# Turned outputs a piece a step, token factors on ScalarE and other orders of loads, in a hybrid mLSTM and DeltaNet block

## The chip, the cores and the metric

One Trainium2 chip, one of its cores. The time is device microseconds (us) of one execution. Before the change the runs took 2233.39, 2235.78 and 2241.74 us, a median of 2235.78.

## The reference

One decoder layer on 512 tokens of width 2048, all in fp32. The two input streams of heads and the merge come from one projection each way:

```python
u = rmsnorm(x, norm_w)
z = u @ w_in                  # q, k, v, gates of mLSTM; q, k, v, gates of DeltaNet; merge gates
h_ml = mlstm(...)             # 8 heads, qk 128, v 256, chunkwise; gated, normalised per head
h_dn = gated_delta(...)       # 16 heads of 128; conv of 4 taps, SiLU, l2norm of q and k, decay
y_ml, y_dn = h_ml @ w_out[:2048], h_dn @ w_out[2048:]
out = rmsnorm(x + sigmoid(g1) * y_ml + sigmoid(g2) * y_dn, final_norm_w)
```

The DeltaNet heads need in each chunk the solution of a lower triangular system (1 + A) X = R, where A is made of the products of the keys, of the decays and of a factor per token.

## The kernel before

**Products.** Each fp32 operand is split into a part that TensorE takes exactly (hi, L135 on ScalarE) and the rest (lo, L138 on VectorE), and each product takes three matmuls: hi hi, hi lo, lo hi. The lines are L261 to L263 in `proj_cm`, L575 to L577 in `seven` and L1306 to L1308 in the wide blocks. Weights come in 256 KB tiles by SP's DMA queue (`wr`, L176), four raw and four split buffers (`wh`, `wl`), split three weights ahead of their use.

**Steps.** TensorE's order is written out by hand. After every six wide matmuls the program calls `tick()`, which advances all the side work, written as Python generators: each `yield n` says that the generator goes on n ticks later, and `start(gen, n)` puts one in. A scheduler puts the other engines' instructions into the order of each engine by priority: `urgent` raises it, and `behind("A")` (or "V", "S") ties an instruction behind the newest split on ScalarE (VectorE), or behind the newest weight load on SP. Each engine then works in order.

**Stages.** (1) 0 to 95 us: x, the norm, u transposed and split. (2) To about 1050: `seven`, a scheme of seven products of half size for eight, in twelve blocks of 77 us. A block has quads A, then quads B; each quad is three weight tiles of 512 columns (`load_quad`, L505, in `wr3`) of which VectorE makes sums. An A quad writes its sum ts to DRAM (`t2_d`, L531), and the B quad of the same rows reads it back as the third of its three tiles and makes `ts = r[0] - r[2]` (L535). (3) 1060 to 1960: eight DeltaNet units of two heads, with the mLSTM heads between them. A unit projects k, v, q (`proj_cm`, copied out by `conv_silu` into `yp`, L770), makes the matrices of the solve (`dn_front_k`), sends them over DRAM (`ld`, `ls`) to the 32x32 layout, runs 31 steps of substitution on VectorE (`tmp`, L881), completes the inverse by four products with copies by ScalarE and VectorE between them (`dn_back`, p1 to p4; the copy of p3 is `s`, L962, which L966 multiplies), then runs the chain over the chunks (`dn_chain`, L990 to L1011). (4) To 2010: the third wide block, with `load_h2`, which loads and splits the DeltaNet outputs, and `lead`, which loads three quads of the next stage and splits the first. (5) 2011 to 2172: two blocks of `seven` for the output projection, whose sums stand in `t2o_d`. (6) To 2232: `last_block`, with the mLSTM outputs (`hmr`, split to `uh` and `ul` by L1180 and L1181), the known parts of y (`hf`, L1427), their squares (L1435) and the final norm.

**Turned outputs.** `turn` transposes a head's output in 32x32 blocks on VectorE into a buffer `to` (two of them), and `travel` sends it to DRAM (`hm_d`, `h_d`) in four pieces of 64 KB (L806). Outputs go by ScalarE's DMA queue, all four pieces in one step; loops inside a unit go by SP's queue. An mLSTM head has two outputs, one step apart.

**Token factors.** Three tiles are multiplied by a factor per token in one VectorE instruction of 128x512 each: `aq` by `cs` (L857, ahead of the solve), `vt` by `nk` (L972, ahead of the chain), `kw` by `we` (L1110, mLSTM).

Of the kernel before, what the change touches and what calls it, by code (L numbers as in the profile page):

```python
# [11 lines left out]
ALU = mybir.AluOpType  # L12
# [3 lines left out]
P = 128  # L16
S = 512
NC = S // P
# [9 lines left out]
YDRAIN = 2  # L28
# [14 lines left out]
BS = 32  # L43
# [12 lines left out]
def hybrid_body(  # L56
# [27 lines left out]
    tg_d = dr.tile([NC, P, 2 * D], F32, tag="tgd", name="tg_d")  # L84
# [47 lines left out]
    newest = {}  # L132
# [7 lines left out]
    def behind(eng):  # L140

        return tc.issue_after(newest[eng])
# [66 lines left out]
    def urgent(level=1):  # L209
        return tc.high_priority(offset=level * PRIO)  # L210
# [6 lines left out]
    def start(gen, wait=0, by=None):  # L217
        active.append([gen, clock["t"] + wait, held["by"] if by is None else by])
# [29 lines left out]
    banks = (((psj, "pj"),) * 3 + ((psw, "wk"),), ((psw, "wk"),) * 2 + ((pso, "o"),) * 2)  # L248
# [235 lines left out]
    def seven_stage(sbp, su, s4, X, t2_d, w_, k0, blocks, sinks, hook):  # L484
# [8 lines left out]
        def load_quad():  # L493
            if len(rawq) == len(quads):
                return
            _, c1, c2, b, g, i = quads[len(rawq)]
            with tc.high_priority(offset=2 * PRIO):
                r = sbp.tile([P, 3, NO], F32, tag="wr3", name="wr3", bufs=3)
                k1, k2 = (slice((k0 + 2 * i + n) * P, (k0 + 2 * i + n + 1) * P) for n in range(2))
                if g == "A":  # L500
                    src = (w_[k1, c1:c1 + NO], w_[k1, c2:c2 + NO], w_[k2, c2:c2 + NO])
                else:
                    src = (w_[k2, c1:c1 + NO], w_[k2, c2:c2 + NO], t2_d[b % 2, i])
                for n in range(3):
                    nc.sync.dma_start(r[:, n, :], src[n])  # L505
            rawq.append(r)

        def split(src, wide):
# [217 lines left out]
    lead, seven = seven_stage(sbp, (suh, sul), (s4h, s4l), X, t2_d, w_in, 0, SEVEN, SINK, begin_mixers)  # L726
# [36 lines left out]
    def bc(col, n):  # L763
        return col.unsqueeze(2).to_broadcast([P, NC, n])
# [27 lines left out]
    def turn(src, dst, out=False, lag=5):  # L792


        o = dst if dst is not src and len(dst.shape) == 3 else wk.tile([P, NC, P], F32, tag="to", name="to", bufs=2)
        V.transpose(o if len(src.shape) == 3 else o.rearrange("p n c -> p (n c)"), src)
        start(travel(o, dst, out), lag if out else 2)

    def travel(o, dst, out):

        d = dst if len(dst.shape) == 4 else dr.tile([16, BS, 4, BS], F32, tag="td", name="td", bufs=8)
        ov = o.rearrange("p n (j c) -> p (n j) c", c=BS)
        q = nc.scalar if out else nc.sync
        with behind("A") if out else urgent(2):
            for a in range(4):
                q.dma_start(d[:, :, a, :].rearrange("m r c -> r m c"), ov[a * BS:(a + 1) * BS])  # L806
        if d is dst:
            return
        yield 4
        with behind("A") if out else urgent(2):  # L810
            q.dma_start(dst, d.rearrange("(n j) r a c -> (j r) n (a c)", n=NC))
        yield 1

    def dn_front_k(hs, kq, u):
# [37 lines left out]
            V.tensor_tensor(out=cs[:, j, :], in0=cs[:, j, :], in1=beta[:, :, hs[j]], op=ALU.mult)  # L852
        u["nk"] = nk
        ld = dr.tile([2 * NC, 4, BS, BS], F32, tag="ld", name="ld", bufs=2)
        for j in range(2):
            aq = u["aq"][j]
            V.tensor_tensor(out=aq[:, :, 0, :], in0=aq[:, :, 0, :], in1=bc(cs[:, j, :], P), op=ALU.mult)  # L857
# [65 lines left out]
    def dn_back(hs, kq, u):  # L923

        tn, tt = u["tn"], u["tt"]
        G2 = [(j * NC + c, u["aq"][j][:, c, 0, :]) for j in range(2) for c in range(NC)]
        for b in range(4):
            bs = slice(b * BS, (b + 1) * BS)
            G.tensor_copy(tb[bs, :, bs], tt[bs])
        for b in range(2):  # L930
            bs = slice(b * BS, (b + 1) * BS)
            G.tensor_copy(ta[bs, :, bs], tn[bs])
        p1 = psw.tile([P, 2 * NC, BS], F32, tag="wk", name="p1")
        for g, a in G2:
            for q in range(2):
                a0, a1 = slice(64 * q, 64 * q + 32), slice(64 * q + 32, 64 * q + 64)
                T.matmul(p1[a1, g, :], a[a0, a1], tn[a0, g, :], start=True, stop=True)
        s1 = wk.tile([P, 2 * NC, BS], F32, tag="s3", name="s1", bufs=1)
        for q in range(2):
            a1 = slice(64 * q + 32, 64 * q + 64)  # L940
            with urgent():
                A.mul(s1[a1], p1[a1], -1.0)
        yield 2
        p2 = psw.tile([P, 2, 2 * NC, BS], F32, tag="wk", name="p2")
        for g, a in G2:
            for q in range(2):
                a0, a1 = slice(64 * q, 64 * q + 32), slice(64 * q + 32, 64 * q + 64)
                T.matmul(p2[a0, 0, g, :], s1[a1, g, :], tt[a1, g, :], start=True, stop=True)
            T.matmul(p2[32:64, 1, g, :], tt[32:64, g, :], s1[32:64, g, :], start=True, stop=True)
        with urgent(2):  # L950
            V.tensor_copy(ta[32:64, :, 0:32], p2[32:64, 1])
        for q in range(2):
            a0, a1 = slice(64 * q, 64 * q + 32), slice(64 * q + 32, 64 * q + 64)
            with urgent():
                A.copy(tb[a0, :, a1], p2[a0, 0])
        yield 3
        p3 = psw.tile([P, 2 * NC, 64], F32, tag="wk", name="p3")
        for g, a in G2:
            T.matmul(p3[64:128, g, :], a[0:64, 64:128], ta[:, g, :], start=True, stop=True)
        s3 = wk.tile([P, 2 * NC, 64], F32, tag="s3", name="s3", bufs=1)  # L960
        with urgent():
            A.mul(s3[64:128], p3[64:128], -1.0)  # L962
        yield 2
        p4 = psw.tile([P, 2 * NC, 64], F32, tag="wk", name="p4")
        for g, a in G2:
            T.matmul(p4[0:64, g, :], s3[64:128, g, :], tb[64:128, g, 64:128], start=True, stop=True)  # L966
        with urgent():
            V.tensor_copy(tb[0:64, :, 64:128], p4[0:64])
        for j in range(2):
            vn = u["vs"][j]  # L970
            with behind("V"):
                V.tensor_tensor(out=vn, in0=vn, in1=bc(u["nk"][:, j, :], P), op=ALU.mult)  # L972
        start(dn_chain(0, hs, kq, u), 2)
        start(dn_chain(1, hs, kq, u), 3)

# [99 lines left out]
    def ml_head(h, kq):  # L1075
# [30 lines left out]
        G.memset(v1[:, :, NB:NB + 1], 1.0)  # L1106
        nc.sync.dma_start(v1[:, :, 0:NB], v_d[:, :, h * NB:(h + 1) * NB].rearrange("c p n -> p c n"))
        yield 6
        with behind("V"):
            V.tensor_tensor(out=kw, in0=kw, in1=bc(we, P), op=ALU.mult)  # L1110
        yield 2

        sq = wk.tile([P, NC], F32, tag="sq", name="sq")
# [257 lines left out]
    X2 = late["X"]  # L1371
# [52 lines left out]
        return (lambda t: put(tgs[11, t], m1[t], t, c1)), end5, end7  # L1424

    def known(c, a, b):
        nc.sync.dma_start(fin["hf"][:, c, a:b], y_d[c, :, a:b])  # L1427

    def put(t, src, c, col, now=True):
        gated(t, src, now)  # L1430
# [94 lines left out]
    def last_block():  # L1525
# [30 lines left out]
        def beside():  # L1556
            yield 2
            for c in range(NC):
                known(c, 0, HD)
                yield 2  # L1560
            nc.sync.dma_start(fw, final_norm_w.partition_broadcast(P))
            yield 2
            for c in range(NC):
                known(c, HD, D)
                nc.sync.dma_start(tgs[c], tg_d[c, :, nsl])
                for n, a in enumerate(range(0, HD, NO)):
                    square(c, a, a + NO, n)
                weigh(c, 0, HD)
                yield 3
                square(c, HD, CT, 2)  # L1570
                weigh(c, HD, CT)
                yield 1
# [34 lines left out]
                    tick()  # L1607
            done_c(c)

    wide_block(YDRAIN, banks[1], lambda c: X2[:, c // 2, c % 2, :], [(load_h2(), 1), (lead(), 18)])  # L1610
    for b, blk in enumerate(OUTS):
        seven(2 * KH * b, *blk)
    last_block()
# [33 lines left out]
```

## Time and profile before

| | |
|---|---|
| runs | 2233.39, 2235.78, 2241.74 us |
| profiled execution | 2233.9 us, span 2232.1 us |
| TensorE | busy 2159.3 us, 97%, mean granted clock 0.994 |
| VectorE | busy 1671.0 us, 75% |
| ScalarE | busy 995.0 us, 45% |
| GpSimd | busy 276.6 us, 12% |
| DMA | 435.81 MB, mean 195 GB/s |

A row of the waits names the waiting instruction, who it waited for, the total, how often and the longest, in us. A row of a timeline has the start, the duration, the engine (ACTq and SPq are DMA issues), the line, the operation and, in brackets, the idle time before it with its releaser. A row of the windows has the stretch, its length, the busy times of TensorE, its weight loads, VectorE, ScalarE and GpSimd with their counts, the granted TensorE clock, the DMA share and GB/s. A row of the groups has the line, engine, operation, shapes and count, the busy us and the mean ns of one, and the idle time before. The profile was taken on one execution; times in it start at the span's start.

### The profile page before, as it was taken

The page shows a single profiled execution, that of the slowest core. Times are in us where ns is not written, and L with a number is a line of the kernel's source. Part 1 is how long each engine was busy: PE and PEld are TensorE (multiplying, and loading weights), DVE is VectorE, ACT ScalarE, POOL GpSimd, SP SyncE. Part 2 cuts the span into 40 slices and gives each one's busy share as a digit, 9 for nine tenths or more (in the row PEclk, how much of TensorE's full clock was granted, in tenths as well). Part 3 has the DMA queues.
Part 4 walks back from the last instruction along what each step waited for, and adds up shares of the span by engine and source line. Part 5 has one row for each costly group of instructions (what it writes and reads, how often), then busy time and mean ns, then how long its engine had stood idle before and what let it go on. Part 6 is the DMA issues. An engine that isn't in the chain of part 4 may idle for free. (4 is left out here: it accounts for less than half of the span.)

```text
span 2232.1 us, 31548 instructions
## 1 busy us (share of the span) xinstructions
PE 2159.3 (97%) x10592; PEld 1771.9 (79%) x10592; DVE 1671.0 (75%) x2907; ACT 995.0 (45%) x1890; POOL 276.6 (12%) x356
## 2 busy tenths in 40 slices
PE   7999999999999999999999999999999999999997
PEld 5877878888788788788878887878888887877775
DVE  5787788888878777877588876757675868667875
ACT  5444444444444343444544544444444445344344
POOL 0320000000000000000222422222222211110101
PEclk9999999999999999999999999999999999999999
DMA  5456666667667766776776767676756568695896
GB/s 156 125 174 193 199 201 201 205 202 231 197 208 228 235 210 205 229 244 192 195 189 168 179 145 174 147 172 166 178 139 167 141 153 230 186 278 184 250 317 215
DMA packets 534821, 435.81 MB, mean 195 GB/s; under 512 B 241921, under 2 KB 393698, under 8 KB 534530
## 3 DMA queue, kind: packets, MB, share of 16 engines
q1 hardware_dynamic: 425058, 357.68, 56.4%
q10 hardware_dynamic: 105568, 68.77, 9.8%
q0 software_dynamic: 4032, 7.34, 2.2%
q8 instruction: 83, 1.36, 0.3%
q14 instruction: 80, 0.66, 0.1%
HBM read 342.37 MB, written 95.49 MB: 196 GB/s over the span
## 5 line engine op out<-in xcount | busy, mean ns | idle before, releaser
L135 ACT CAST wh<-wr 128x512 fp32r<-128x512 f32 (+1 forms) x538 | 379.9, 707 | 470.9 <-PE pj L262 261.8
L138 DVE TENSOR_TENSOR wl<-wr,wh 128x512 fp32r<-128x512 f32 (+1 forms) x538 | 447.2, 834 | 178.2 <-ACT wh L135 160.2
L261 PE MATMUL pj<-uh,wh 128*128 128x512 f32 x1024 | 431.6, 421 | 4.2 <-ACT yp L770 4.2
L263 PE MATMUL pj<-uh,wl 128*128 128x512 f32 x1024 | 404.3, 395 | 0.0
L262 PE MATMUL pj<-ul,wh 128*128 128x512 f32 x1024 | 403.2, 394 | 0.0
L576 PE MATMUL ps<-wl,uh 128*128 128x512 f32 x704 | 277.3, 394 | 7.2 <-DVE wl L138 7.0
L575 PE MATMUL ps<-wh,uh 128*128 128x512 f32 x704 | 276.3, 392 | 7.0 <-DVE X L617 6.5
L577 PE MATMUL ps<-wh,ul 128*128 128x512 f32 x704 | 275.0, 391 | 0.0
L135 ACT CAST wh<-ts 128x512 fp32r<-128x512 f32 x224 | 138.2, 617 | 256.3 <-DVE ts L535 192.2
L135 ACT CAST wh<-t 128x1024 fp32r<-128x1024 f32 x112 | 117.9, 1053 | 250.9 <-PE ps L577 122.8
L263 PEld LDWEIGHTS pj<-uh,wl 128*128 128x128 f32 x1024 | 194.1, 190 | 43.3
L261 PEld LDWEIGHTS pj<-uh,wh 128*128 128x128 f32 x1024 | 195.2, 191 | 40.8 <-ACT yp L770 5.4
L576 PE MATMUL ps<-wl,suh 128*128 128x512 f32 x576 | 224.2, 389 | 1.6 <-DVE wl L138 1.6
L575 PE MATMUL ps<-wh,suh 128*128 128x512 f32 x576 | 224.5, 390 | 0.8 <-ACT qk L353 0.3
L577 PE MATMUL ps<-wh,sul 128*128 128x512 f32 x576 | 224.1, 389 | 0.0
L262 PEld LDWEIGHTS pj<-ul,wh 128*128 128x128 f32 x1024 | 195.6, 191 | 33.4
L138 DVE TENSOR_TENSOR wl<-ts,wh 128x512 fp32r<-128x512 f32 x224 | 153.6, 689 | 38.0 <-ACT wh L135 38.0
L138 DVE TENSOR_TENSOR wl<-t,wh 128x1024 fp32r<-128x1024 f32 x112 | 137.6, 1229 | 48.0 <-ACT wh L135 47.4
L576 PEld LDWEIGHTS ps<-wl,uh 128*128 128x128 f32 x704 | 132.6, 188 | 43.1 <-DVE wl L138 16.7
L575 PEld LDWEIGHTS ps<-wh,uh 128*128 128x128 f32 x704 | 132.5, 188 | 40.5 <-DVE X L617 12.7
L577 PEld LDWEIGHTS ps<-wh,ul 128*128 128x128 f32 x704 | 132.5, 188 | 26.7
L535 DVE TENSOR_TENSOR ts<-wr 128x512 f32<-128x512 f32 x112 | 77.2, 690 | 99.8 <-DMA wr<-t_d 76.0
(302 smaller groups left out, 3462.5 us busy)
## 6 DMA issues: line engine op xcount, KB each, us to landing
wr<-in_w_in_dram SPq DMA_DIRECT2D x704, 256.0 KB, 3.7
wr<-in_w_out_dram SPq DMA_DIRECT2D x138, 256.0 KB, 4.8
t_d<-ts ACTq DMA_DIRECT2D x96, 256.0 KB, 4.4
wr<-t_d SPq DMA_DIRECT2D x96, 256.0 KB, 4.1
wr<-in_w_in_dram SPq DMA_DIRECT2D x64, 128.0 KB, 3.2
xt<-in_x_dram SPq DMA_DIRECT2D x8, 512.0 KB, 7.2
tg_d<-X ACTq DMA_DIRECT2D x16, 256.0 KB, 6.1
tg_d<-to ACTq DMA_DIRECT2D x16, 256.0 KB, 5.1
```

Of the source, the lines that this page charges most:

```text
L135: newest["A"] = A.copy(hi, src).ins
L138: newest["V"] = V.tensor_tensor(out=lo, in0=src, in1=hi.bitcast(F32), op=ALU.subtract).ins
L261: T.matmul(ps[j], hi[:, k, wsl], uh[:, kt, :], start=(kt == 0), stop=False)
L262: T.matmul(ps[j], hi[:, k, wsl], ul[:, kt, :], start=False, stop=False)
L263: T.matmul(ps[j], lo[:, k, wsl], uh[:, kt, :], start=False, stop=(kt == KT - 1))
L535: V.tensor_tensor(out=ts[:, 0, :], in0=r[:, 0, :], in1=r[:, 2, :], op=ALU.subtract)
L575: T.matmul(ps[t], ah, hi, start=(g == "A" and i == 0), stop=False, skip_group_check=True)
L576: T.matmul(ps[t], ah, lo, start=False, stop=False, skip_group_check=True)
L577: T.matmul(ps[t], al, hi, start=False, stop=(i == KH - 1), skip_group_check=True)
```

## The change

Seven edits:

- `travel` sends an output that leaves (by ScalarE's queue) a piece a step, each piece tied behind the newest ScalarE split of its step; the last unit's, with a lag of 3, still go in one step. The two outputs of an mLSTM head are turned four steps apart, not one.
- The factors of `aq`, `vt` and `kw` are put in by ScalarE, four multiplications of 128x128 for each tile of 128x512. Those of `aq` come one step later, and the wait ahead of the substitution is a step shorter, so the loop starts at the same step.
- In a quad, the tiles are loaded in the order first, third, second.
- The loads of `hf`, `fw` and of the last gates are tied behind the newest weight load on SP, and quad and tail loads now count as weight loads.
- `lead` starts 8 steps into the third wide block, not 18.

```diff
@@ load_quad (seven_stage)
-                for n in range(3):
-                    nc.sync.dma_start(r[:, n, :], src[n])
+                for n in (0, 2, 1):
+                    newest["S"] = nc.sync.dma_start(r[:, n, :], src[n]).ins
@@ turn, travel
-        start(travel(o, dst, out), lag if out else 2)
+        start(travel(o, dst, out, lag > 3), lag if out else 2)
...
-        q = nc.scalar if out else nc.sync
-        with behind("A") if out else urgent(2):
+        if out:
             for a in range(4):
-                q.dma_start(d[:, :, a, :].rearrange("m r c -> r m c"), ov[a * BS:(a + 1) * BS])
-        if d is dst:
+                with behind("A"):
+                    nc.scalar.dma_start(d[:, :, a, :].rearrange("m r c -> r m c"), ov[a * BS:(a + 1) * BS])
+                if apart:
+                    yield 1
             return
@@ dn_front_k
+        yield 1
         for j in range(2):
             aq = u["aq"][j]
-            V.tensor_tensor(out=aq[:, :, 0, :], in0=aq[:, :, 0, :], in1=bc(cs[:, j, :], P), op=ALU.mult)
+            with urgent():
+                for c in range(NC):
+                    A.mul(aq[:, c, 0, :], aq[:, c, 0, :], cs[:, j, c:c + 1])
...
-        yield 10
+        yield 9
@@ dn_back
-            with behind("V"):
-                V.tensor_tensor(out=vn, in0=vn, in1=bc(u["nk"][:, j, :], P), op=ALU.mult)
+            with behind("A"):
+                for c in range(NC):
+                    A.mul(vn[:, c, :], vn[:, c, :], u["nk"][:, j, c:c + 1])
@@ ml_head
-        with behind("V"):
-            V.tensor_tensor(out=kw, in0=kw, in1=bc(we, P), op=ALU.mult)
+        with behind("A"):
+            for c in range(NC):
+                A.mul(kw[:, c, :], kw[:, c, :], we[:, c:c + 1])
...
             turn(g[i], hm_d[2 * h + i], True)
-            yield 1
+            yield 4
@@ known; the same tie for fw and tgs in last_block
-        nc.sync.dma_start(fin["hf"][:, c, a:b], y_d[c, :, a:b])
+        with behind("S"):
+            nc.sync.dma_start(fin["hf"][:, c, a:b], y_d[c, :, a:b])
@@ load_tail
-                    nc.sync.dma_start(r[:, i, :], w_out[k * P:(k + 1) * P, nsl])
+                    newest["S"] = nc.sync.dma_start(r[:, i, :], w_out[k * P:(k + 1) * P, nsl]).ins
@@ the third wide block
-    wide_block(YDRAIN, ..., [(load_h2(), 1), (lead(), 18)])
+    wide_block(YDRAIN, ..., [(load_h2(), 1), (lead(), 8)])
```

Line numbers behind L805 are larger in the changed kernel: L962 becomes L969, L955 becomes L962, L1180 becomes L1189, L1427 becomes L1437, L1447 becomes L1457.

On ScalarE, in the DeltaNet unit around 1460 us, before (`hm_d<-to` are the pieces of an mLSTM head's two outputs, `s` from 64x512 is the copy that L966 multiplies, `yp` the copy of a projection):

```order
L135 CAST wh<-wr 128x512
L806 DMA hm_d<-to 32x16x32 x4
L955 COPY tb<-p_14727 32x8x32 x2
L135 CAST wh<-wr 128x512
L806 DMA hm_d<-to 32x16x32 x3
L135 CAST wh<-wr 128x512
L806 DMA hm_d<-to 32x16x32
L962 ACTIVATE s_14798<-p_14789 64x512
L770 COPY yp_9097<-pj 128x512
```

The same place of the changed kernel:

```order
L135 CAST wh<-wr 128x512
L806 DMA hm_d<-to 32x16x32
L962 COPY tb<-p_14799 32x8x32 x2
L135 CAST wh<-wr 128x512
L806 DMA hm_d<-to 32x16x32 x2
L135 CAST wh<-wr 128x512
L806 DMA hm_d<-to 32x16x32
L980 ACTIVATE vt<-vt,nk 128x128 x2
L969 ACTIVATE s_14864<-p_14855 64x512
L980 ACTIVATE vt<-vt,nk 128x128 x6
L806 DMA hm_d<-to 32x16x32
L770 COPY yp_9097<-pj 128x512
```

Four pieces in place of eight stand ahead of s, two factors of vt stand ahead of it and six behind it. In two other units all eight factors of vt stand ahead of s.

On SP, from the third B quad of the last `seven` block, before (`wr_20436` and its like are quads, `hf`, `fw` and `hmr` as above):

```order
L1447 DMA hmr<-hm_d 128x4x128 x2
L1427 DMA hf<-y_d 128x1024 x3
L505 DMA wr_20436<-in_w_out_dram 128x512 x2
L505 DMA wr_20436<-t2o_d 128x512
L1427 DMA hf<-y_d 128x1024
L1561 DMA fw<-in_final_norm_w_dram 128x2048
L505 DMA wr_20476<-in_w_out_dram 128x512 x2
```

And the end of SP's list in the changed kernel (`wrt` are the six tail weights, `wr` at L176 the ten others of `last_block`, `X` the last gates):

```order
L1548 DMA wrt<-in_w_out_dram 128x512 x6
L176 DMA wr<-in_w_out_dram 128x512
L1572 DMA fw<-in_final_norm_w_dram 128x2048
L1577 DMA X_19104<-tg_d 128x512 x2
L176 DMA wr<-in_w_out_dram 128x512 x4
L1437 DMA hf<-y_d 128x1024
L176 DMA wr<-in_w_out_dram 128x512
L1437 DMA hf<-y_d 128x1024 x2
L176 DMA wr<-in_w_out_dram 128x512
L1437 DMA hf<-y_d 128x1024
```

All eight loads of `hf` now stand behind the seventh weight of L176; four of them and `fw` stood among the quads.

On ScalarE at the end of the third wide block, before (`wh<-ts` and `wh<-wr_19213` are the casts of `lead`, which take the wide weights' buffers):

```order
L135 CAST wh<-wr 128x512
L1180 ACTIVATE uh<-hr,normc 128x512
L135 CAST wh<-ts 128x512
L1180 ACTIVATE uh<-hr,normc 128x512
L1180 ACTIVATE tu<-hsum,normc 128x768
L1245 DMA he_d<-hs 128x512
L135 CAST wh<-wr_19213 128x512
L1180 ACTIVATE uh<-hr,normc 128x512 x2
L135 CAST wh<-wr 128x512
```

The same casts in the changed kernel:

```order
L135 CAST wh<-ts 128x512
L531 DMA t2o_d<-ts 128x512
L1189 ACTIVATE uh<-hr,normc 128x512 x2
L135 CAST wh<-wr_19210 128x512
L1189 ACTIVATE uh<-hr,normc 128x512 x2
L135 CAST wh<-wr 128x512
L531 DMA t2o_d<-ts 128x512
L135 CAST wh<-wr 128x512
L1189 ACTIVATE uh<-hr,normc 128x512
L135 CAST wh<-wr 128x512 x2
```

The two casts of `lead` came one wide weight ahead of the block's end and come six ahead of it now.

More of the change, by code (lines that the diff above doesn't have):

```diff
@@ L1560, in beside @@
                 yield 2
-            nc.sync.dma_start(fw, final_norm_w.partition_broadcast(P))
+            with behind("S"):
+                nc.sync.dma_start(fw, final_norm_w.partition_broadcast(P))
             yield 2
@@ L1564, in beside @@
                 known(c, HD, D)
-                nc.sync.dma_start(tgs[c], tg_d[c, :, nsl])
+                with behind("S"):
+                    nc.sync.dma_start(tgs[c], tg_d[c, :, nsl])
                 for n, a in enumerate(range(0, HD, NO)):
@@ L1608, in last_block @@
             done_c(c)
-    wide_block(YDRAIN, banks[1], lambda c: X2[:, c // 2, c % 2, :], [(load_h2(), 1), (lead(), 18)])
+    wide_block(YDRAIN, banks[1], lambda c: X2[:, c // 2, c % 2, :], [(load_h2(), 1), (lead(), 8)])
     for b, blk in enumerate(OUTS):
```

9 lines of the change are left out of this document (6 added, 3 removed).

## The prediction

> **What bounds the kernel now.** I read the busy shares at the top of the page first.
>
> ```profile
> span 2232.1 us, 31548 instructions
> PE 2159.3 (97%) x10592; PEld 1771.9 (79%) x10592; DVE 1671.0 (75%) x2907; ACT 995.0 (45%) x1890; POOL 276.6 (12%) x356
> ```
>
> TensorE is busy 2159.3 of 2232.1 us, so all that a change can win without taking matmuls away lies in the other 72.8 us and in stretches at a lower clock. The change leaves TensorE's list as it is, row for row, so only waits can move. The second view is TensorE's own waits between 1060 and 1960 us, the stage of the eight DeltaNet units (total, times, longest):
>
> ```profile
> PE p L966 <- ACT s L962: 7.8, 4, 2.6
> PE pj L261 <- ACT yp L770: 4.2, 3, 2.1
> PE pr L990 <- DVE st L1009: 2.4, 1, 2.4
> PE py L1306 <- ACT yp L770: 2.3, 2, 1.7
> ```
>
> Three of the four are waits for ScalarE, an engine that is 45% busy. Its timeline where the longest one ends says why (start, duration, what; ACTq rows are DMA issues):
>
> ```profile
> 1455.62 4.44 ACTq L806 DMA_DIRECT2D hm_d<-to  x4
> ...
> 1463.13 0.93 ACTq L806 DMA_DIRECT2D hm_d<-to  x2
> ...
> 1465.01 0.31 ACTq L806 DMA_DIRECT2D hm_d<-to  x1
> 1465.42 0.59 ACT L962 ACTIVATE s<-p 64x512 f32<-64x512 f32 x1 [0.63 <-DMA wr<-in_w_in_dram]
> 1466.04 0.59 ACT L770 COPY yp<-pj 128x512 f32<-128x512 f32 x1
> ```
>
> ScalarE works in order. Four pieces of a turned output in a row hold it for 4.44 us, 1.1 each, four more follow between casts and copies, the last one alone for 0.31, and the negated product s (L962), for which TensorE's L966 waits, starts only at 1465.42. The same stands ahead of the copy yp in the first unit:
>
> ```profile
> 1132.32 5.60 ACTq L806 DMA_DIRECT2D hm_d<-to  x3
> 1137.96 0.59 ACT L770 COPY yp<-pj 128x512 f32<-128x512 f32 x1 [5.08 <-DMA v<-v_d]
> ```
>
> Here three issues take 5.60 us and yp comes 5.08 us late. The third view is the stretches around the stalls; the column after the five busy times is the granted clock:
>
> ```profile
> 1136.00:1144.00 8.00, 5.93 (x20) 4.38 (x19) 4.54 (x12) 4.71 (x10) 0.00 (x0) 0.79 1.12 243
> 1384.00:1393.00 9.00, 6.58 (x27) 5.16 (x26) 5.89 (x26) 1.88 (x6) 0.19 (x1) 0.81 0.60 147
> 1462.00:1472.00 10.00, 7.41 (x38) 5.85 (x37) 6.66 (x11) 4.68 (x8) 1.52 (x2) 0.83 0.91 236
> 1575.00:1583.00 8.00, 6.33 (x40) 5.05 (x40) 5.51 (x9) 5.32 (x11) 1.28 (x2) 1.00 0.98 263
> 1685.00:1694.00 9.00, 7.75 (x40) 6.07 (x39) 6.64 (x10) 4.88 (x9) 0.90 (x2) 0.81 0.92 233
> 1797.00:1806.00 9.00, 6.75 (x35) 5.23 (x34) 6.13 (x10) 4.36 (x8) 0.00 (x0) 0.81 0.66 167
> 2135.00:2144.00 9.00, 6.45 (x22) 4.85 (x21) 5.64 (x8) 2.61 (x3) 0.00 (x0) 0.81 1.02 377
> ```
>
> A stall often costs twice. In the first stretch 0.21 of 8 us is clock not granted, that is 1.7 us; in the 9 us ones 0.19 x 9, again 1.7. Of the four stalls at L966 three lose it and the one at 1575 does not.
>
> **Turned outputs, a piece a step.** In the order of the changed kernel the unit at 1460 has 1, 2 and 1 pieces between the copies ahead of s where it had 4, 3 and 1, and the others follow s and yp. A step is six matmuls, about 1.4 us, and a lone piece costs 0.31 us, as in the row at 1465.01, not 1.1. Of the 7.8 us at L966 I take back 6.8 (one of four stalls keeps 1 us, since four pieces still stand ahead). The three falls of the clock there go: 3 x 1.7 = 5.1. Of the 4.2 us at L261 the stall of 2.1 goes and half of the rest, 3.1, and with it the fall at 1136, 1.7. The 2.3 us at L1306 stay: they belong to the last unit, whose outputs have a lag of 3 and are not taken apart. Together **-16.7**. The two buffers of turned outputs are held three or four steps longer; VectorE's transposes need one per head and output, which come tens of us apart, so I count nothing for it; were the cover gone, it would be a VectorE wait of about a step, 1.4 us.
>
> **Token factors on ScalarE.** What goes and the nearest row for what comes:
>
> ```profile
> L972 DVE TENSOR_TENSOR vt<-vt,nk 128x512 f32<-128x512 f32 x16 | 12.0, 789 | 0.0
> L857 DVE TENSOR_TENSOR aq<-aq,cs 128x512 f32<-128x512 f32 x16 | 10.3, 689 | 0.0
> L1110 DVE TENSOR_TENSOR kw<-kw,we 128x512 f32<-128x512 f32 x8 | 5.5, 684 | 0.0
> L828 ACT ACTIVATE dm<-dm,ngam 128x128 f32<-128x128 f32 x64 | 20.2, 387 | 0.0
> ```
>
> VectorE loses 27.8 us of work. ScalarE gets 40 x 4 = 160 multiplications of 128x128; 20.2 us for 64 is 0.32 each, so 50 us, or 6.3 per unit. It has 1237 us idle, so most hides; what counts is where it stands in an in-order queue. Eight factors of vt (2.5 us) stand just ahead of s in two units, and eight of aq wait there for the reciprocal on VectorE with the weight casts behind them. The factors of aq also feed the loads of the solve, a step later than before:
>
> ```profile
> DVE tmp L881 <- DMA ls<-ld: 11.1, 2, 7.0
> ```
>
> Two units already wait there, 11.1 us, and the longer one ends in the 2.4 us at L990 and the fall at 1384. The loop still starts at the same step, so a later load is a longer wait. Bounds: from -4.1 (that stall and its fall gone, as VectorE is freer) to +50 (nothing hidden). I take **+4**: about 1 us in each of the two units with vt ahead of s and in each of the two that wait for ls, near the low end since idle time is 24 times the added work.
>
> **Sums reloaded second of three.** VectorE's waits where a quad's weight sum is read back, and the issue slot on SP's queue:
>
> ```profile
> DVE ts L535 <- DMA wr<-t_d: 76.0, 47, 4.6
> 2124.75 0.43 SPq L505 DMA_DIRECT2D wr<-t2o_d  x1
> ```
>
> The sum now goes out one slot, 0.43 us, earlier, and the weight loaded last is not needed first. TensorE feels this only where the accumulation stands behind the waiting ts on VectorE:
>
> ```profile
> PE ps L575 <- DVE X L617: 2.5, 3, 2.0
> ```
>
> That is between 100 and 1060 us: three stalls by 0.43 give **-1.3** (0 to -2.5; if the slot is given back, ts waits for r0 in its place).
>
> **Late loads behind weights.** The stall near the end:
>
> ```profile
> 2131.49 0.93 SPq L1447 DMA_DIRECT2D hmr<-hm_d  x2
> 2132.47 3.03 SPq L1427 DMA_DIRECT2D hf<-y_d  x3
> 2135.60 2.10 SPq L505 DMA_DIRECT2D wr<-in_w_out_dram  x2
> 2138.07 0.33 SPq L505 DMA_DIRECT2D wr<-t2o_d  x1
> 2138.18 0.69 DVE L535 TENSOR_TENSOR ts<-wr 128x512 f32<-128x512 f32 x1 [3.37 <-DMA wr<-t2o_d]
> PE ps L575 <- DVE X L617: 4.0, 2, 2.5
> ```
>
> Three loads of hf stand 3.03 us on SP ahead of a quad, whose sum arrives 3.37 us late with TensorE's accumulation behind it: a stall of 2.5 and the fall of 1.7 in the stretch at 2135. After, hf stands behind the seventh of the last ten weights. **-4.2** (0 if the load of the sum is late for the two hmr loads, which stay).
>
> But four halves of hf (0.5 MB each, 2.1 MB) and fw are added to a later time:
>
> ```profile
> 2190.00:2195.00 5.00, 5.00 (x24) 4.11 (x22) 1.05 (x3) 1.08 (x2) 0.00 (x0) 1.00 1.07 342
> 2195.00:2200.00 5.00, 4.16 (x17) 2.93 (x16) 4.46 (x7) 4.45 (x12) 0.00 (x0) 1.00 1.01 371
> 2200.00:2205.00 5.00, 4.27 (x19) 3.19 (x17) 3.19 (x6) 3.57 (x8) 0.00 (x0) 1.00 0.48 144
> PE py L1306 <- ACT uh L1180: 1.1, 1, 1.1
> ```
>
> At 371 GB/s, 2.1 MB take 5.7 us, in a time when the engines are full; from 2200 on there is room for (371 - 144) x 5 = 1.1 MB in 5 us, about half. The square of hf stands in ScalarE's queue among the last casts and the uh that TensorE already waits for. I take **+2.5**, the half that does not fit, with bounds of 0 and 8 (all 5.7 and both late operands doubled).
>
> **The lead ten steps earlier.** Its splits now take two of the four weight buffers before the last six weights of the third wide block, not before the last one or two. The waits for splits from 1960 us on:
>
> ```profile
> PE py L1307 <- DVE wl L138: 2.9, 5, 1.3
> PE py L1306 <- ACT wh L135: 2.4, 2, 2.0
> ```
>
> 5.3 us in seven stalls with four buffers mostly free; half as much again is **+3** (0 to 8, six weights at the longest 1.3).
>
> **Sum.** -16.7 + 4 - 1.3 - 4.2 + 2.5 + 3 = -12.7. The profiled execution took 2233.9 us (a span of 2232.1 and 1.8 around it), 1.9 under the median of 2235.8; the sum is made against it: 2221.2, which I round to **2221**.
>
> **A rule beside the clock row.** The stretches at 1462, 1685 and 1797 lose clock after stalls of at most 2.6 us. The Trainium skill, in "TensorE: Matmul & The Clock Gate", Part 1, under "What's actually happening", says that half clock comes after at least one idle window of about 3.4 us. By it no stall here is long enough, the falls would have another cause than these stalls, and the forecast would lack their gain; the trace speaks against it so far, with falls within 2 us of six stalls, though the stall at 1575 shows none.
>
> **Rivals.** *The stalls only move.* The pieces are as many as before, four still precede s, and if they now delay yp instead, half of the 16.7 is lost: 2221 + 8.4 = 2229.6. For it: yp copies are waited for already. Against: the lone pieces cost 0.31 us. Or the change spaces the pieces in the program only and a piece still waits for its lane; the time is the same. *The falls come from elsewhere.* The five falls counted stay: 5 x 1.7 = 8.5, so 2229.7. *The solve comes late (slower).* The factors of aq leave ScalarE over 1 us later, the loads land behind the loop's start, VectorE waits with weight splits behind it, and each unit gets what one has now, the 2.4 us at L990 and a fall of 1.7. In seven more units that is 28.7: 2221.2 + 28.7 = 2249.9. It decides once ls lands over about 1 us later than now. For it: two units wait already. Against: six show no wait. *Everything hides.* No cost for factors, lead and hf, and the stall at L990 with its fall gone: 2221.2 - 9.5 - 4.1 = 2207.6.
>
> **How the numbers follow.** A measurement of this kernel can tell about 0.5% from no change: 2224.6 to 2247.0. Chances: forecast 0.46, moved stalls 0.20, falls from elsewhere 0.06, late solve 0.14, all hidden 0.14. Faster than 2224.6: 0.40 of the forecast's share (its own range is 2213 to 2229) and all hidden, 0.54; same: 0.06 + 0.20 + 0.06 = 0.32; slower 0.14. The range runs from all hidden, with 1.6 us below, to just under the late solve: 2206 to 2248.
>
> **What would show it.** Right: no wait of over 1 us at the matmul behind the negated product, full clock in the four stretches, ScalarE about 50 us busier and VectorE 28 less, no stall at 2136. Wrong: yp waited for instead, waits for ls in more than two units, more waits for wl and wh between 1980 and 2010, or waits for uh after 2185 of over 5 us in all.

## The result, and the profile after

The changed kernel is slower: a median of 2246.75 us (2242.52 to 2256.46, six runs) against 2233.17 us before (2226.53 to 2241.74, six runs), a ratio of 1.0067 with a 95% interval of 1.0048 to 1.0087. That is 15 us more (11 to 19) where 12.7 less was forecast: inside the range given, but on the other side of no change. The profiled execution took 2253.09 us, 6 above the median, so places are read from it and sizes from the timed runs.

The busy shares of the changed kernel:

```profile
span 2251.3 us, 31740 instructions
PE 2175.0 (97%) x10592; PEld 1774.3 (79%) x10592; DVE 1641.8 (73%) x2867; ACT 1040.9 (46%) x2050; POOL 266.3 (12%) x356
```

The work moved as counted: VectorE has 29 us less, ScalarE 46 more. TensorE's busy time rose by 15.7 us with the same 10592 matmuls. Part of that is clock, as these stretches of the changed kernel show (length, five busy times, granted clock, DMA share, GB/s):

```profile
1855.00:1865.00 10.00, 7.38 (x20) 5.70 (x21) 9.36 (x23) 6.92 (x13) 0.00 (x0) 0.66 1.03 287
1988.00:2001.00 13.00, 7.73 (x22) 5.54 (x21) 8.29 (x13) 5.45 (x9) 0.00 (x0) 0.74 1.06 372
2171.00:2182.00 11.00, 8.27 (x23) 5.96 (x22) 6.71 (x9) 5.91 (x9) 0.00 (x0) 0.69 0.92 308
2204.00:2213.00 9.00, 6.51 (x20) 4.50 (x20) 3.67 (x6) 4.80 (x11) 0.00 (x0) 0.81 0.99 292
```

The last three stand behind the units, with a fourth of 1.7 us at 2225, where before had one fall, at 2140; the three cost 3.4, 3.4 and 1.7 us of clock. In the units the changed kernel has four falls: at 1389, 1577 and 1690, of 1.7 us each, and the first row's, of 3.4. They cost 8.5 us, as much as the five of before. TensorE's waits in the unit stage (1060 to 1960 us) of the changed kernel:

```profile
PE p L973 <- ACT s L969: 5.9, 4, 2.6
PE py L1315 <- ACT yp L770: 3.5, 1, 3.5
PE pr L998 <- DVE st L1017: 3.1, 1, 3.1
PE pj L261 <- ACT yp L770: 0.4, 1, 0.4
```

The stage became better, but less than forecast: the wait ahead of L261 nearly went (4.2 to 0.4), the one for s only fell from 7.8 to 5.9, and the waits at pr (2.4 to 3.1) and of the last unit (2.3 to 3.5) grew. After 1960 us:

```profile
PE py L1315 <- ACT wh L135: 6.2, 2, 4.1
PE ps L576 <- DVE wl L138: 5.1, 6, 1.5
PE ps L575 <- ACT wh L135: 3.6, 2, 2.1
```

Here 6.2 stands where 2.4 stood, 5.1 where 1.6 stood, and the third row is new. (The waits for X at L617, with the stall of 2136, fell from 4.0 to 1.5.) Since TensorE's order is the same in both, its n-th matmuls can be set side by side. The changed kernel's n-th matmul starts 6.7 us later than before's at 1055, 0.2 earlier at 1960, 4.5 later at 2011, 13.6 at 2172 and 19.2 at 2221. So about 7 us were lost in the first stage of `seven`, where the forecast had a gain of 1.3, 7 won in the units, 5 lost at the third wide block, 9 in the last `seven` blocks, 6 at the end. Stage by stage such differences between two single profiles carry up to 7 us of chance: two kernels below, with the lists of before up to 1960 us, stand 2 and 5 us ahead of its profile at 1055, and one with the lists of before in the units (the new load order alone) loses 7 us there.

### The profile page after: what moved, and what is told of

Its sections match the earlier page's. It is cut to its first block, busy times and chain, and to the rows that moved or that the text cites. A ratio compares the mean times of both kernels' runs of the same rounds, so it can differ in the third digit from the quotient of the medians.

```text
span 2251.3 us, 31740 instructions
## 1 busy us (share of the span) xinstructions
PE 2175.0 (97%) x10592; PEld 1774.3 (79%) x10592; DVE 1641.8 (73%) x2867; ACT 1040.9 (46%) x2050; POOL 266.3 (12%) x356
## 5 line engine op out<-in xcount | busy, mean ns | idle before, releaser
L261 PE MATMUL pj<-uh,wh 128*128 128x512 f32 x1024 | 430.2, 420 | 0.4 <-ACT yp L770 0.4
L261 PEld LDWEIGHTS pj<-uh,wh 128*128 128x128 f32 x1024 | 194.4, 190 | 36.6 <-ACT yp L770 1.0
L535 DVE TENSOR_TENSOR ts<-wr 128x512 f32<-128x512 f32 x112 | 77.4, 691 | 147.1 <-DMA wr<-t_d 112.1
L576 PEld LDWEIGHTS ps<-wl,uh 128*128 128x128 f32 x704 | 132.8, 189 | 44.1 <-DVE wl L138 18.8
```

The source lines that it names most:

```text
L261: T.matmul(ps[j], hi[:, k, wsl], uh[:, kt, :], start=(kt == 0), stop=False)
L535: V.tensor_tensor(out=ts[:, 0, :], in0=r[:, 0, :], in1=r[:, 2, :], op=ALU.subtract)
L576: T.matmul(ps[t], ah, lo, start=False, stop=False, skip_group_check=True)
```

## The experiments

First each part alone on the kernel before. All were timed in five rounds beside the kernel before on the same chip, whose medians were 2233 to 2235 us; a difference in us is the ratio less one by 2234.

**Turned outputs alone** (`travel` and the four steps between an mLSTM head's outputs).

> Only the turned outputs a piece a step, and the four steps between the two outputs of an mLSTM head; all else as before. Theory (the places add up): between 1060 and 1960 us the changed kernel gained 6.9 us, with the factors' cost in it. Alone the pieces then gain that and what the factors cost, 8 to 12 us, a ratio of about 0.995 to 0.996, and the waits at the matmul behind the negated product fall well below the 7.8 us of before. Rival (the stalls only moved): the waits for s go and waits for yp come, the gain is under 4 us, a ratio of 0.998 to 1.0.

Measured: 0.9973 (0.9961 to 0.9985), 6.0 us faster. It lies between the two ranges, and neither had the places right: both expected the waits for s to fall, and they did not; the waits for yp ahead of L261, 4.2 us before, are the ones that went.

```profile
PE p L970 <- ACT s L966: 8.1, 4, 2.9
PE pr L994 <- DVE st L1013: 3.6, 1, 3.6
PE py L1310 <- ACT yp L770: 2.7, 1, 2.7
```

The waits for s are 8.1 us, 7.8 before, with five pieces ahead of s in place of eight. ScalarE in this kernel, where s is late by 3 us:

```profile
1552.63 3.12 ACTq L806 DMA_DIRECT2D hm_d<-to  x2
1555.92 0.62 ACT L135 CAST wh<-wr 128x512 fp32r<-128x512 f32 x1 [2.75 <-DMA hm_d<-to]
1559.57 2.06 ACTq L806 DMA_DIRECT2D hm_d<-to  x2
1561.73 0.59 ACT L966 ACTIVATE s<-p 64x512 f32<-64x512 f32 x1 [5.19 <-DMA hm_d<-to]
```

Two pieces take 3.12 and two take 2.06 us. A lane here is the semaphore by which a transfer tells of its landing; the program gives SP's and ScalarE's issues eight of them in common, and an issue waits on its engine until the earlier user of its lane has landed. In this trace the four issues start at 1552.63, 1555.35, 1559.57 and 1561.32 us, each within 0.03 us of such a landing: of the output's piece before, and of three loads that SP had issued (`gb`, `nrb` and `v`). Spacing the pieces by a step did not spare them that wait: over the whole run ScalarE's pieces wait 34 us for earlier transfers, 47 before, and weight loads are 7 of the 34.

**Factors alone.**

> Only the three token factors on ScalarE, those of aq a step later; all else as before. Theory (the places add up): a cost of 2 to 5 us, since the pieces in a row still hold ScalarE and the eight factors of vt stand between them and s in two units; a ratio of 1.001 to 1.002. Rival (ScalarE's idle time hides them and VectorE's 28 us help): 0 to -3 us. Second rival (the solve comes late): waits for ls in most units and about 29 us more, a ratio of 1.013.

Measured: 1.0015 (1.0005 to 1.0025), 3.4 us slower, as the theory had it. The solve is not the cause: VectorE's waits for ls are 6.9 us in three places here, 11.1 in two before. TensorE's waits for s (7.8 to 9.1 us) and for yp ahead of L261 (4.2 to 5.6) are longer by 2.7 together in the profile. The row of the new work in the changed kernel (its like for `aq` has a mean of 389, for `kw` of 392) bears out the size:

```profile
L980 ACT ACTIVATE vt<-vt,nk 128x128 f32<-128x128 f32 x64 | 20.2, 390 | 12.1 <-DMA nrb<-rows_d 7.7 <-DMA iwb<-rows_d 3.3 <-DMA ke<-td 0.9
```

**The new load order alone.**

```diff
-                for n in range(3):
+                for n in (0, 2, 1):
                     nc.sync.dma_start(r[:, n, :], src[n])
```

> Only the order first, third, second of a quad's three loads; all else as before. Theory (the sum ts, expected one load earlier, moves ahead of VectorE's other work and waits there for the read-back with the accumulations and weight splits behind it): VectorE's waits for the read-back grow from 76 to over 100 us between 100 and 1060 us, and the time grows by 6 to 10 us, a ratio of 1.003 to 1.0045. Rival (that growth in the changed kernel's profile is variation of one execution, 6 us above its median): within 2 us of before, 0.999 to 1.001. Forecast of the prediction: -1.3 us.

Measured: 1.0065 (1.0046 to 1.0084), 14.5 us slower, by itself as much as the whole change. In VectorE's order 28 of the 96 sums ts of the first stage's B quads now stand one or two splits further ahead; the others stand where they stood. Kernel before, at the fourth and fifth sums of a block:

```profile
810.60 0.69 DVE L535 TENSOR_TENSOR ts<-wr 128x512 f32<-128x512 f32 x1 [0.26 <-DMA wr<-t_d]
812.03 0.69 DVE L138 TENSOR_TENSOR wl<-ts,wh 128x512 fp32r<-128x512 f32 x1 [0.74 <-ACT wh L135]
812.98 1.23 DVE L138 TENSOR_TENSOR wl<-wr,wh 128x1024 fp32r<-128x1024 f32 x1 [0.26 <-ACT wh L135]
814.89 0.69 DVE L535 TENSOR_TENSOR ts<-wr 128x512 f32<-128x512 f32 x1 [0.68 <-DMA wr<-t_d]
```

The same place with the new order:

```profile
811.60 0.69 DVE L138 TENSOR_TENSOR wl<-ts,wh 128x512 fp32r<-128x512 f32 x1 [0.74 <-ACT wh L135]
813.85 0.69 DVE L535 TENSOR_TENSOR ts<-wr 128x512 f32<-128x512 f32 x1 [1.56 <-DMA wr<-t_d]
814.46 1.22 DVE L138 TENSOR_TENSOR wl<-wr,wh 128x1024 fp32r<-128x1024 f32 x1
```

Before, the split of the pair (128x1024) ran at 812.98 and then ts waited. Now ts stands ahead of it, waits 1.56 us for its read-back, and the split begins at 814.46: TensorE, which is due for it, loses 1.8 us there. Most losses are smaller. Between 350 and 1050 us the gaps of 0.1 to 0.3 us in TensorE's list are 28 before and 68 here, those of 0.3 to 1 us 10 and 16. In the two output blocks 7 of the 16 sums moved ahead as well, and there the n-th matmul falls 10 us further behind that of before, between 1960 and 2136 us. (This profile took 2255.06 us, 10 above the kernel's median.)

**The lead alone**, 8 for 18.

> Only the lead 8 steps into the third wide block in place of 18; all else as before. Theory (its sums and splits wait for their loads on VectorE and ScalarE with the wide weights' splits behind them): one stall of 4 us or more between 1980 and 2000 us and a fall of the clock, 5 to 8 us more, a ratio of 1.002 to 1.0035. Rival (the stall of the changed kernel comes from the new order and ties of the loads in that stage, not from the lead's place): within 2 us of before and no stall over 2.5 us there.

Measured: 1.0019 (1.0006 to 1.0033), 4.2 us slower, just under the range expected, with one stall of 4.2 us at 1988 and a fall of the clock behind it. VectorE in the changed kernel, which has the same stall:

```profile
1980.42 1.23 DVE L528 TENSOR_TENSOR t<-wr 128x1024 f32<-128x1024 f32 x1 [5.12 <-DMA wr<-in_w_out_dram]
1981.56 0.68 DVE L138 TENSOR_TENSOR wl<-wr,wh 128x512 fp32r<-128x512 f32 x1
```

The lead's sum t waits 5.12 us for its load on VectorE with a wide weight's split behind it. TensorE's stall comes 7 us later, at a cast, and how the one leads to the other was not followed.

**The late loads alone.**

> Only the ties of the late loads (hf, fw, the last gates) behind the newest weight load, with quad and tail loads counted as such; all else as before. Theory (the places add up): the other four parts measured -6, +3.4, +14.5 and +4.2 us, 16.1 together, the whole change +14, so this part is near -2 us: what the stall at 2136 us gives back (4.2) less what the later loads of hf cost at the end. A ratio of 0.998 to 1.0. Rival (the loads of hf collide with the last weights and hmr): 5 to 9 us more, as the changed kernel's profile shows from 2172 us on, a ratio of 1.002 to 1.004.

Measured: 1.0040 (1.0026 to 1.0055), 8.9 us slower: the rival. The waits of ScalarE from 2180 us on, before:

```profile
ACT uh L1180 <- DMA hmr<-hm_d: 10.9, 4, 4.5
ACT wh L135 <- DMA wr<-in_w_out_dram: 1.6, 2, 1.3
```

In this kernel:

```profile
ACT wh L135 <- DMA wr<-in_w_out_dram: 9.2, 3, 4.6
ACT uh L1180 <- DMA hmr<-hm_d: 8.9, 3, 4.4
...
ACT jk L1436 <- DMA hf<-y_d: 3.6, 1, 3.6
```

The waits for the last weights grew from 1.6 to 9.2 us and one for hf is new; the waits for hmr did not grow. Nor was the stall at 2136 won: with the three loads of hf gone from ahead of that quad, its read-back still comes late and TensorE's same matmul still loses 1.8 us there, 2.7 before. Another stall stands 26 us behind it, in the last B quad, whose sum now comes among the first weights of the last block, the tail weights and the hmr loads:

```profile
2169.24 0.69 DVE L535 TENSOR_TENSOR ts<-wr 128x512 f32<-128x512 f32 x1 [4.65 <-DMA wr<-t2o_d]
```

TensorE loses 2.4 us there.

Next, what makes each part cost.

**The new load order with ts tied.** The only edit beside the order: the sum waits for its turn on VectorE.

```diff
+            if g == "B":
+                for key in ((0, q - 1), (1, q - 2)):
+                    if key in slo:
+                        ties.enter_context(tc.issue_after(slo[key]))
...
+                    with ties:
+                        V.tensor_tensor(out=ts[:, 0, :], in0=r[:, 0, :], in1=r[:, 2, :], op=ALU.subtract)
...
+                    slo[0, q] = newest["V"]
```

Here `slo` holds the newest low split after a quad's sum (0) and after its pair (1).

> The loads of a quad in the order first, third, second, all else as before, but VectorE's sum ts of a B quad is tied behind the split of the quad's before (its sum) and of the one two before (its pair), about where it stood before the change. Theory (ts standing ahead of splits and accumulations on VectorE is what costs): the 14.5 us of the order alone go down to 0 to 4, a ratio to before of 1.0 to 1.002, and stalls of 0.1 to 0.3 us on TensorE between 350 and 1050 us come back to about 30 from 68. Rival (the order of the loads itself costs, since the pair's second tile now lands last): 8 to 15 us remain, 1.0035 to 1.0065.

Measured: 0.9934 (0.9919 to 0.9949), 14.7 us faster than before. The cost is gone and more with it, which neither expected. The tie does not put ts just where it was: against before, 20 of the 96 sums stand one or two splits further back. The row of the windows counts it, TensorE's matmuls between 350 and 1040 us. Before:

```profile
350.00:1040.00 690.00, 684.15 (x2992) 559.33 (x2991) 548.90 (x692) 312.75 (x450) 0.86 (x8) 1.00 0.70 218
```

With the new order alone:

```profile
350.00:1040.00 690.00, 683.43 (x2961) 551.73 (x2960) 544.31 (x688) 311.07 (x448) 0.85 (x8) 1.00 0.68 215
```

With the new order and the tie:

```profile
350.00:1040.00 690.00, 689.96 (x3044) 570.69 (x3043) 556.73 (x700) 316.95 (x458) 0.86 (x8) 1.00 0.69 219
```

In the same 690 us 2961 matmuls, 2992 or 3044: at 0.227 us from one to the next, 31 fewer are 7 us and 52 more are 12 us. With the tie only two gaps of over 0.1 us are left. VectorE's waits in this stage (100 to 1060 us) say where they went; with the tie:

```profile
DVE wl L138 <- ACT wh L135: 133.5, 190, 2.0
DVE ts L541 <- DMA wr<-t_d: 35.1, 35, 2.9
```

In the changed kernel:

```profile
DVE ts L535 <- DMA wr<-t_d: 112.1, 63, 3.9
DVE wl L138 <- ACT wh L135: 71.4, 108, 2.3
```

A wait of a sum for its read-back (76.0 before, 112.1, 35.1) holds splits that are due. The wait of splits for their casts is longest in the fastest of these kernels, so it held little that TensorE was due for.

**The tie alone, with the old load order.**

> The kernel before with its load order (first, second, third) and only the tie of the sum ts behind the split of the quad's before and the pair's two before; VectorE's list in the twelve blocks is the same as with the new load order and the tie. Theory (the place of ts on VectorE decides, the load order little): the gain of 14.3 us that the tie with the new order gave stays within 4, a ratio of 0.9925 to 0.9955. Rival (the new load order is what gains once ts cannot run ahead): 0 to -5 us, 0.998 to 1.0.

Measured: 0.9961 (0.9937 to 0.9984), 8.7 us faster, between the two ranges. The place of ts is most of the gain: this kernel has 3033 matmuls in the 690 us, 41 more than before, where the tie with the new order has 52 more. The intervals with and without the new order overlap, so whether that order adds some 5 us once ts is tied is not settled.

**The lead's loads early, its sums where they were.** The lead gets ten steps of waiting between its loads and its sums.

> The lead starts 8 steps into the third wide block, but only its loads: its sums and splits stay where they stood before (24 steps in); all else as before. Theory (the early sums wait for their loads on VectorE and ScalarE and hold the wide weights' splits): the 4.2 us of the early lead go, a ratio of 0.999 to 1.001, and no stall over 2.5 us between 1985 and 2000 us. Rival (the early loads take SP's queue and the DMA engines from the wide weights): the cost stays, 1.0015 to 1.0025.

Measured: 1.0002 (0.9989 to 1.0015). The cost is gone in the median. But the profile keeps a stall of 4.0 us at 1999 (2.1 before at this place), so the second half of what was expected failed; that the early sums cost, and not the early loads, is likely and not shown beyond the two intervals, which just overlap.

**Outputs by GpSimd's queue**, all four pieces in one step, on the kernel before.

```diff
-        q = nc.scalar if out else nc.sync
+        q = nc.gpsimd if out else nc.sync
```

> Turned outputs that leave go by GpSimd's DMA queue, four pieces in one step as before, so that ScalarE issues none of them between 1100 and 1970 us; all else as before. Theory (ScalarE is held by issues that wait for an earlier user of their lane, so it is the issues' place on ScalarE that costs, not that they come in a row): the waits for s (7.8 us), for yp ahead of L261 (4.2) and L1306 (2.3) and most falls of the clock there go, and the gain is 12 to 17 us, a ratio of 0.9925 to 0.9945, two to three times what a piece a step gave. Rival (something else holds s, as the waits of 8.1 us in the kernel with pieces apart could say): the waits for s stay over 5 us and the gain is under 6. Second rival (GpSimd, which makes the chain's factors, is held in ScalarE's place): new waits for GpSimd and no gain.

Measured: 0.9921 (0.9909 to 0.9934), 17.6 us faster. TensorE's waits between 1060 and 1950 us are now only these:

```profile
PE pr L990 <- DVE st L1009: 6.3, 2, 4.0
PE py L1306 <- ACT yp L770: 2.7, 2, 2.2
```

No wait for s and none ahead of L261. That the pieces came in a row was not the point; that ScalarE's queue took them was. The run does not part what goes with that: GpSimd's issues have eight lanes of their own, on which the pieces wait 0.4 us for earlier transfers in all, and the same bytes go in 471335 packets, not 534821. The four falls of the clock behind those stalls went as well. Two are left in the units, behind the wait of 4.0 us at pr and behind the one of the last unit, the second twice as long:

```profile
1378.00:1386.00 8.00, 5.37 (x23) 4.65 (x24) 5.88 (x26) 0.56 (x2) 0.19 (x1) 0.79 0.53 147
1839.00:1849.00 10.00, 8.13 (x22) 5.96 (x23) 9.17 (x19) 6.78 (x12) 0.39 (x1) 0.66 1.00 305
```

They cost 1.7 and 3.4 us, 5.1 in place of 8.5.

**The changed kernel with the tie.**

> The changed kernel whole, with only the tie of ts added. Theory (ts ahead on VectorE is the largest part of its loss): it falls by 22 to 30 us, from 1.0065 of before to 0.993 to 0.997, and stalls between 350 and 1050 us nearly vanish. Rival (the parts overlap, since alone they sum to +25 and together give +14): it falls by 10 to 16 us and stays at 0.999 to 1.002.

Measured: 0.9904 (0.9882 to 0.9926), 21 us faster than before and 36 below the changed kernel, more than either expected.

**Pairs.** Turned outputs and factors together:

> Two parts of the change together: outputs a piece a step and the factors on ScalarE; all else as before. Apart they measured -6.0 and +3.4. Theory (parts of the same stage overlap, since the five parts alone sum to +25 and the whole gives +14): together -8 or better, a ratio of 0.9965 or below. Rival (they add): -2.6 within 2, 0.998 to 0.9998, and the surplus lies in other pairs or in the spread of the single measurements.

Measured: 0.9952 (0.9935 to 0.9969), 10.7 us faster, where -6.0 and +3.4 would add to -2.6. They overlap; beside the turned outputs the factors do not cost what they cost alone. Its waits:

```profile
PE p L973 <- ACT s L969: 4.4, 3, 1.9
PE py L1315 <- ACT yp L770: 3.4, 2, 3.1
PE pr L998 <- DVE st L1017: 2.7, 1, 2.7
```

The wait for s falls to 4.4 us, from 8.1 with the pieces alone: in its list the factors of vt stand among the pieces, and four pieces precede s, not five. With this pair, the three other parts give -10.7 + 14.5 + 4.2 + 8.9 = 17, against 15 measured with an interval of 11 to 19.

**The late loads without what waits for them.**

> The late loads alone (9.0 us slower than before), and the squares of hf on ScalarE and its products with fw on VectorE, columns 0 to 1535, left out, so that nothing on those two engines waits for hf before the end; the loads stay. The output lacks both. Theory (squares that wait for hf hold the casts and the uh behind them on ScalarE): 6 to 9 us come back, a ratio to before of 0.999 to 1.0015, and the stalls between 2195 and 2210 us are under 1.5 us together. Rival (the loads of hf crowd out hmr and the last weights on the DMA engines): 4 us or more remain, 1.002 or above, with the wait for hmr still over 3 us.

Measured: 1.0040 (1.0024 to 1.0056), 8.9 us: all of the cost remains and the theory falls. ScalarE's waits from 2180 us:

```profile
ACT uh L1180 <- DMA hmr<-hm_d: 16.1, 4, 9.1
ACT wh L135 <- DMA wr<-in_w_out_dram: 9.0, 4, 5.3
```

No square waits for hf any more, and the waits for hmr have grown instead, to 16.1.

**The late loads with half the bytes.**

> The late loads alone (9.0 us slower than before), but each of the eight loads of hf brings only half of its columns, 2.1 MB less in all, and hf is set to zero ahead of it, so the output lacks the other half; the number and the place of the loads on SP stay. Theory (the bytes of hf crowd out the last weights and hmr on the DMA engines after 2185 us): about half of the cost or more goes, 1.000 to 1.0025. Rival (the place on SP's queue ahead of the last three weights costs, whatever the bytes): the cost stays, 1.003 to 1.005.

Measured: 1.0017 (1.0002 to 1.0031), 3.8 us: about half is left, as the bytes would have it, though the interval just overlaps that of the late loads alone. ScalarE's waits, where the loads still stand ahead of the last three weights:

```profile
ACT uh L1180 <- DMA hmr<-hm_d: 5.6, 4, 2.9
ACT wh L135 <- DMA wr<-in_w_out_dram: 2.4, 1, 2.4
```

**The two gains together**, outputs by GpSimd's queue, new load order, tie:

> The two that gained, put together on the kernel before: outputs by GpSimd's queue (-17.3 us alone) and the new load order with ts tied (-14.3 alone). Theory (they act in different stages and add): -28 to -33 us, a ratio of 0.985 to 0.9875. Rival (a shared limit, DMA or the clock): under -24, above 0.989.

Measured: 0.9856 (0.9836 to 0.9876), 2203.48 us. They add.

**And with the factors:**

> The best so far (outputs by GpSimd's queue, new load order with ts tied, 0.9856 of before) with the factors on ScalarE added. Theory (with the issues gone from ScalarE, its idle time hides the factors, and VectorE, which ends the waits of the chain at pr, is relieved of 28 us): equal or up to 6 us faster, 0.983 to 0.986. Rival (the factors cost here what they cost alone, 3.4 us): 0.9865 to 0.988.

Measured: 0.9848 (0.9831 to 0.9866), 2200.52 us: not to be told from the one without them. It is the fastest kernel of this study, 1.5% below before and 2% below the change. Its waits between 1060 and 1950 us show what is left:

```profile
PE pr L1002 <- DVE st L1021: 6.9, 3, 3.2
PE py L1319 <- ACT yp L778: 3.0, 2, 2.3
PE p L977 <- ACT s L973: 2.4, 2, 1.6
```

## Why the prediction was wrong

| term of the sum | forecast | measured alone |
|---|---|---|
| turned outputs | -16.7 | -6.0 |
| factors | +4 | +3.4 |
| load order | -1.3 | +14.5 |
| late loads: stall at 2136 and end | -4.2 + 2.5 | +8.9 |
| lead | +3 | +4.2 |
| sum | -12.7 | +25, as a whole +15 |

**The step that failed first is the load order**, and with it the sign. The prediction took the edit as a transfer that lands a slot earlier, "three stalls by 0.43", and counted on SP's queue only. What the scheduler makes of a load that it expects earlier stands in VectorE's list, and the list of the changed kernel had it: 28 of the 96 sums one or two splits further ahead. The quoted row of 76.0 us of waits for the read-back was the warning. A wait of that size on an in-order engine is harmless only as long as nothing due stands behind it. The tie shows the place as the cause: the same loads with ts behind are 14.7 us faster than before, so 29 us hang on where some of these sums, of 0.69 us each, stand.

**The turned outputs** had the right cause and the wrong cure. Their place on ScalarE's queue did cost 17.6 us, as the kernel with GpSimd's queue shows; the forecast was 16.7. The step that failed is "a lone piece costs 0.31 us". That row was one piece that found its lane free. A piece waits for the lane's earlier user, and four of the five pieces ahead of s in the rows above still hold it for 1.0 to 1.6 us each. The second form of the first rival, "a piece still waits for its lane", had this, but was given a part of 0.20.

**The late loads** were wrong twice. Freeing the queue at 2136 left 1.8 of the 2.7 us there, and a stall of 2.4 came at 2169, so the 4.2 us were not won. And the bytes: 2.1 MB of hf less took 5.1 of the 8.9 us away, near the estimate of 5.7; the assumption that half would fit was not borne out, and the last weights pay, whose waits grew from 1.6 to 9.2 us. The cost of 8.9 lies above the upper bound of 8, with an interval (5.8 to 12.3) that holds it.

**The factors and the lead** came in size as counted. The factors' cost is an addend only alone: with the turned outputs it does not show, so the sum's form failed there. The lead's size is in part luck: the stall stands where its sums wait for their loads on VectorE, not at the shared buffers that the forecast priced, as far as the runs tell. The slower rival named, a late solve, did not occur. The slower outcome came by a mechanism that was not on the list.

**The clock.** The prediction put 6.8 of the 16.7 us on falls that go with their stalls; the changed kernel lost 8.5 us to falls in the units, as before. A stall does not bring a fall with certainty. The stall of 1.9 us at 134, which all seventeen profiles have, is followed within 1.3 us by a fall in nine of them and by none in eight. Five kernels above that leave the units' lists as they were (the new order, with and without the tie, the tie alone, the lead, and its loads early) lose 6.8 to 13.6 us there, so 8.5 or 5.1 in one profile says little of the size. The rival that the falls have another cause is not borne out: where GpSimd's queue took away the stalls of 1.4 to 2.8 us at L261 and L966, the falls behind them went as well. So in this kernel stalls below the 3.4 us that the Trainium skill names ("TensorE: Matmul & The Clock Gate", Part 1, under "What's actually happening") can cost clock.

**Open**: why the changed kernel with the tie is 21 us faster than before when the measured pair and single parts give -10.7 - 14.7 + 4.2 + 8.9 = -12. The gap of 9 is at the edge of what five such intervals leave. Open too is what of the 17.6 us comes from ScalarE's time, from the lanes or from fewer packets, and how the lead's early sums make the stall at 1988.

## What to carry to other kernels

An edit of a load's order is an edit of every list that waits for it: read the order of the engines behind it, and look for instructions that now wait with due work behind them. On an in-order engine, tie what waits for memory behind what is ready, and let an engine that nothing due stands behind issue the transfers. A piece of a transfer costs its issuer the wait for its lane (1.0 to 1.6 us a piece here), and not only its issue slot (0.31).

## What the runs showed of the hardware

Short gaps weigh more than the list of waits shows. Between 350 and 1050 us TensorE's starts lost 11 us before in gaps of 0.1 us and more, 18 with the new order and 0.3 with the tie, and only 1.8 us of the 18 were in a gap of over 1 us. The list of TensorE's waits has 5.5 us before and 5.0 with the new order between 350 and 1040 us.

Stalls of one length can cost clock or not. That of 1.9 us in the first stage is followed by a fall in the nine profiles in which it ends between 132.8 and 133.8 us, and by none in the eight in which it ends between 134.0 and 134.4. Each fall that begins ahead of the last matmul lasted 3.4 or 6.8 us, at half the clock.

GpSimd issued the 128 pieces at the cost of 93 us of its own busy time (276.6 to 369.3); the wait of TensorE in the units that grew most beside it is that at pr, from 2.4 to 6.3 us.
